# Encoder layer: the embedding gate's products in another order and by token tiles, softmax division inside the probability turn

## The chip, the cores and the metric

The kernel runs on one core of one Trainium2 chip. The metric is the device time of one launch in microseconds (us). The core has a TensorE (PE, with its weight loads as PEld), a VectorE (DVE), a ScalarE (ACT), a GpSimd (POOL) and a SyncE (SP, which here only issues DMAs). A text "L659" is line 659 of the kernel before.

## The reference

One layer on 1024 tokens of width 1024, all in float32:

```python
u = x @ w_in                                  # 2816 columns: rq, rk, rv, rg, aq, ak, av
y_ret = swish(rg) * group_norm(retention_fwd + retention_bwd)      # 8 heads, chunks of 128
y_att = softmax(window scores + alibi, with a sink logit) @ v      # 8 query, 2 key heads, blocks of 128
h = layer_norm(ALPHA * x + concat(y_ret, y_att) @ w_out)           # LN1
g = sigmoid(h @ w_ple_gate)                                        # the embedding gate
f = (silu(h @ w_ffn_gate) * (h @ w_ffn_up)) @ w_ffn_down
out = layer_norm(ALPHA * h + f + g * (p @ w_ple_proj))             # LN2
```

## The kernel before

**Arithmetic.** Large products run in a pair of shorter floats: `split` (L78-80) copies an operand on ACT to a rounded high part and subtracts on DVE for the low part, and `mm3` or `mm3c` (L83-85, L277-279) does three 512-column products for one. The in-projection, the gate, and the FFN's up and down products use a scheme that replaces the eight block products of a 2 by 2 block matrix by seven; its operands are sums of blocks, and its results are sums of products.

**Stages.** In order: the in-projection ("dense" stage, up to about 170 us), attention and retention (to 410), w_out with LN1 (to 505), the embedding gate `ple` (to 606), the FFN's gate and up products (units of four weight tiles; to about 1035), and the down product with LN2.

**Attention and retention.** Heads go in four pairs. For a pair, PE's order is written out by hand as a list of steps given to `run`: K and C are the retention's keys and their products with values (`Retention.keys`, `kv`), Q, Y, N, X its scores, outputs, norms and turns, sco(n), trn(n) and val(n) the scores, the turn and the values of attention block n (`Attention`). F is a place for filler work: `run` takes 28 steps of three products each from one queue (the rest of the in-projection and p @ w_ple_proj) and deals them over the F of a pair, in 28 groups. Only PE is ordered by hand here; a scheduler places the other engines' instructions. Scores of a block: PE, a DVE step that adds the mask and takes the maximum (L651), an ACT exponential with its sum, a DVE reciprocal, and a DVE multiplication of the 128 x 384 scores by the reciprocal (L659, 64 of them). A turn transposes the two heads' scores on PE (L667, 176 blocks of 128 x 128), into PSUM banks that `tbank` (L465) takes in rotation from "t", "t" and "mm"; "mm" is also the fillers' bank. ACT copies the result to SBUF (ptr, L669), and the values multiply it (L679). Before the first pair's scores, `first_keys` (L403) makes rounded copies of its queries and keys, 12 on ACT and 8 on DVE. `weight_sums` (L414) makes sums of the gate's weight blocks on POOL and stores them to DRAM (wsd).

**Gate.** `to_hT` (L846) transposes the normalised tokens (accs) and splits them into HB: four tiles, by half of the features and half of the tokens. `pg` (L921) loads half of a product's weights and splits them, on DVE and POOL in turn. `prod` (L949) runs one of the seven products, with the 128 rows of weights as the outer loop, four PSUM banks open, and side work between. The order is 3, 7, 1, 6, 2, 5, 4; Tokens 4 to 7 are the first block row; they are transposed beside product 7, and tokens 0 to 3, the second block row, inside the w_out loop. Sums of token blocks (`less`, TT) are DVE and POOL steps over 1024 columns of SBUF tiles. `embed_next` (L979) multiplies one gate tile by an embedding tile fetched from DRAM (pe<-ed) and adds the product to zd in DRAM; there are 16 of these, two buffers for the fetched tiles, and each use issues the next fetch on SP. Those left after the gate go one to an FFN unit. After `ple`, `ahead(2, 4)` loads and splits the first FFN weights (in_w_gu, L1088). From the gate on, all engines are ordered as the code is written.

Of the kernel before, what the change touches and what calls it, by code (L numbers as in the profile page):

```python
# [40 lines left out]
def layer(tc, xT, xn, w_first, w_mt, w_out, w_pg, w_pe, pT, w_gu, w_dn,  # L41
# [341 lines left out]
    def slope(i, g):  # L383
        return 2.0 ** -(i + 4 * g + 1)

    def conv_q(i, raw):

        qs = [bt([P, S], "aq", 3, F32R) for _ in range(2)]
        for c in hs:
            for g in range(2):  # L390
                sc_ = 0.125 / slope(i, g)
                a = slice(64 * g, 64 * g + 64)
                z = slice(64 * (1 - g), 64 * (1 - g) + 64)
                act.activation(qs[g][a, c], raw[a, c], AF.Copy, scale=sc_)
                dve.scalar_tensor_tensor(qs[g][z, c], raw[a, c], sc_, qs[g][a, c].bitcast(F32), ALU.mult, ALU.subtract)
        return qs

    k1 = [bt([P, S], f"k1{g}", dt=F32R) for g in range(2)]
    kz = [bt([P, S], f"kz{g}", dt=F32R) for g in range(2)]
    pairs = [[first[2], first[3], None]]  # L400
    for g in range(2):
        pool.memset(kz[g][64 * (1 - g):64 * (1 - g) + 64, :].bitcast(F32), 0.0)

    def first_keys():
        pairs[0][2] = conv_q(0, first[0])
        for c in hs:
            for g in range(2):
                a = slice(64 * g, 64 * g + 64)
                z = slice(64 * (1 - g), 64 * (1 - g) + 64)
                act.activation(k1[g][a, c], first[1][a, c], AF.Copy)  # L410
                dve.tensor_tensor(kz[g][a, c], first[1][a, c], k1[g][a, c].bitcast(F32), ALU.subtract)
                act.activation(k1[g][z, c], first[1][a, c], AF.Copy)
# [1202 lines left out]
```

## Time and profile before

| | |
|---|---|
| runs shown | 1275.48, 1268.9, 1267.56 us (median 1268.9) |
| profiled execution | 1273.47 us, span 1270.5 us, granted clock 0.980 |
| busy over the span | PE 1200.0, DVE 797.3, ACT 509.5, POOL 505.0 us |
| attention (168 to 410) | PE busy 221.41 of 242 us |
| gate and FFN start (505.7 to 663.3) | PE busy 119.88 of 157.6 us |

The profile is of one execution, whose time stands beside its span. Busy time over the whole span is an average over stages with different limits; the stages are read one by one below. In a row of an instruction, out<-in are the program's names; in a group's row follow the count, the busy time, the mean time of one in ns, and the idle time ahead of it with what ended it.

### The profile page before, as it was taken

The page shows a single profiled execution, that of the slowest core. Times are in us where ns is not written, and L with a number is a line of the kernel's source. Part 1 is how long each engine was busy: PE and PEld are TensorE (multiplying, and loading weights), DVE is VectorE, ACT ScalarE, POOL GpSimd, SP SyncE. Part 2 cuts the span into 40 slices and gives each one's busy share as a digit, 9 for nine tenths or more (in the row PEclk, how much of TensorE's full clock was granted, in tenths as well). Part 3 has the DMA queues.
Part 4 walks back from the last instruction along what each step waited for, and adds up shares of the span by engine and source line. Part 5 has one row for each costly group of instructions (what it writes and reads, how often), then busy time and mean ns, then how long its engine had stood idle before and what let it go on. Part 6 is the DMA issues. An engine that isn't in the chain of part 4 may idle for free.

```text
span 1270.5 us, 16734 instructions
## 1 busy us (share of the span) xinstructions
PE 1200.0 (94%) x5899; PEld 988.1 (78%) x5899; DVE 797.3 (63%) x1339; ACT 509.5 (40%) x954; POOL 505.0 (40%) x436
## 2 busy tenths in 40 slices
PE   9999979999999999997669999999999999999997
PEld 7778868787787887775458888888888888888886
DVE  7854377877685477576555455554455546875568
ACT  5432365555656312524413333332333324653442
POOL 2553023332211023226557556556556615034235
PEclk9999989999999999998889999999999999999999
DMA  5223342452311323223673322233332248999986
GB/s 216 87 99 116 122 165 79 167 199 76 126 34 67 116 100 116 100 100 93 175 163 124 125 107 78 76 112 124 125 109 75 80 155 239 373 293 220 251 202 198
DMA packets 72675, 177.40 MB, mean 140 GB/s; under 512 B 8592, under 2 KB 10768, under 8 KB 72592
## 3 DMA queue, kind: packets, MB, share of 16 engines
q1 hardware_dynamic: 61648, 155.37, 34.6%
q0 software_dynamic: 10944, 20.98, 9.6%
q8 instruction: 46, 0.75, 0.2%
q14 instruction: 37, 0.30, 0.1%
HBM read 123.10 MB, written 47.97 MB: 135 GB/s over the span
## 4 chain that ended last, share of the span: by engine, by line
PE 78%; DVE 9%; DMA 6%; ACT 3%; issue 3%; POOL 2%; SPq 0%; DVEq 0%; ACTq 0%; POOLq 0%
PE bs L279 5%; PE bs L277 5%; PE bo L277 5%; PE bs L278 5%; PE bo L279 5%; PE bo L278 5%; PE bmm L277 5%; PE bmm L278 5%; PE bmm L279 5%; PE bt L279 5%; PE bt L277 5%; PE bt L278 5%; PE bmm L83 3%; PE bmm L84 3%; PE bmm L85 2%
## 5 line engine op out<-in xcount | busy, mean ns | idle before, releaser
L1126 POOL TENSOR_TENSOR ev<-ev 128x512 f32<-128x512 f32 x33 | 54.6, 1655 | 91.4 <-DVE ev L1141 38.1
L80 DVE TENSOR_TENSOR w<-raw,w 128x512 fp32r<-128x512 f32 x53 | 47.3, 903 | 54.3 <-ACT w L79 54.2
L80 DVE TENSOR_TENSOR w<-H,w 128x512 fp32r<-128x512 f32 x44 | 41.1, 935 | 61.7 <-ACT w L79 61.7
L646 POOL COPY sc<-skb 128x1 f32<-128x1 f32 x64 | 17.3, 279 | 132.5 <-PE bt L667 45.6
L1096 POOL TENSOR_TENSOR H<-ln 128x512 f32<-128x512 f32 x22 | 28.7, 1306 | 89.3 <-DMA ln<-in_w_gu 89.3
L1130 POOL TENSOR_TENSOR ev<-ev,ev 128x512 f32<-128x512 f32 x44 | 62.7, 1437 | 2.6
L1124 ACT ACTIVATE ev<-ev 128x512 f32<-128x512 f32 x33 | 20.9, 632 | 101.9 <-DVE ev L1141 101.9
L80 DVE TENSOR_TENSOR u<-H,u 128x512 fp32r<-128x512 f32 x47 | 36.5, 776 | 37.4 <-ACT u L79 37.1
L83 PE MATMUL bmm<-H,w 128*128 128x512 f32 x112 | 49.9, 445 | 0.1
L79 ACT ACTIVATE w<-raw 128x512 fp32r<-128x512 f32 x53 | 32.5, 624 | 43.0 <-DMA raw<-in_w_gu 16.7
L655 ACT ACTIVATE sc<-sc,st 128x385 f32<-128x385 f32 (+1 forms) x64 | 37.1, 584 | 25.4 <-DVE st L653 19.6
L79 ACT ACTIVATE u<-H 128x512 fp32r<-128x512 f32 x47 | 29.6, 630 | 44.1 <-POOL H L1097 10.1
L85 PE MATMUL bmm<-H,w 128*128 128x512 f32 x112 | 44.6, 398 | 0.0
L84 PE MATMUL bmm<-H,w 128*128 128x512 f32 x112 | 44.5, 397 | 0.0
L832 POOL TENSOR_TENSOR stt<-stt,cst 128x1 f32<-128x1 f32 x8 | 11.6, 1451 | 76.7 <-DVE stt L831 70.0
L80 DVE TENSOR_TENSOR u<-raw,u 128x512 fp32r<-128x512 f32 x30 | 35.3, 1177 | 10.2 <-ACT u L79 10.2
L651 DVE CUSTOM_DVE_ANT_0 sc<-cst,bs,skb 128x384 f32<-128x384 f32 (+1 forms) x64 | 35.0, 574 | 5.0 <-PE bs L650 5.0
L1100 POOL TENSOR_TENSOR H<-raw,H 128x512 f32<-128x512 f32 x22 | 37.8, 1717 | 0.0
L79 ACT ACTIVATE w<-H 128x512 fp32r<-128x512 f32 x44 | 27.4, 622 | 22.1 <-PE bs L279 7.5
L1097 POOL TENSOR_TENSOR H<-H,raw 128x512 f32<-128x512 f32 x22 | 35.1, 1594 | 1.7
L1246 POOL DMA_DIRECT2D h0b<-in_w_dn x24 | 21.3, 900 | 31.6 <-issue 18.4
L1246 POOL DMA_DIRECT2D H<-in_w_dn x11 | 9.6, 872 | 58.3 <-DMA H<-in_w_dn 51.9
(813 smaller groups left out, 4171.6 us busy)
## 6 DMA issues: line engine op xcount, KB each, us to landing
ad<-ev SPq DMA_DIRECT2D x33, 512.0 KB, 2.6
raw<-in_w_gu SPq DMA_DIRECT2D x22, 512.0 KB, 4.4
ln<-in_w_gu SPq DMA_DIRECT2D x22, 512.0 KB, 3.6
raw<-ad SPq DMA_DIRECT2D x40, 256.0 KB, 6.0
ln<-ad SPq DMA_DIRECT2D x37, 256.0 KB, 6.4
H<-in_w_dn SPq DMA_DIRECT2D x33, 256.0 KB, 6.7
raw<-in_w_mt SPq DMA_DIRECT2D x12, 512.0 KB, 3.5
h0b<-in_w_dn POOLq DMA_DIRECT2D x24, 256.0 KB, 6.8
```

Of the source, the lines that this page charges most:

```text
L79: act.activation(hi, raw, AF.Copy)
L80: dve.tensor_tensor(lo, raw, hi.bitcast(F32), ALU.subtract)
L83: pe.matmul(o, lh, rh, start=start, stop=False)
L84: pe.matmul(o, lh, rl, start=False, stop=False)
L85: pe.matmul(o, ll, rh, start=False, stop=stop)
L277: pe.matmul(o, lh, rh, start=start, stop=False, skip_group_check=True)
L278: pe.matmul(o, lh, rl, start=False, stop=False, skip_group_check=True)
L279: pe.matmul(o, ll, rh, start=False, stop=stop, skip_group_check=True)
L655: act.activation(sc[g][:, :nk + 1], sc[g][:, :nk + 1], AF.Exp, bias=st_[:, 1, j, g:g + 1], accum_out=st_[:, 2, j, g:g + 1])
L1100: pool.tensor_tensor(s[3], a(0, 1), s[0], ALU.subtract)
L1126: pool.tensor_tensor(c[:, 1, :], c[:, 0, :], c[:, 1, :], ALU.mult)
L1130: pool.tensor_tensor(self.ev[dst][:, 0, :], left, right, op)
```

## The change

The gate's products run in the order 1, 2, 6, 7, 5, 4, 3, with the token tile as outer loop, so a tile's result is final before the next tile's begins, and its sum or sigmoid follows at once (`post`). HB of tokens 0 to 3 is the first block row. For tokens 4 to 7, `to_T` forms the block sums of one tile from the PSUM transposes while products 1 and 2 run. LN1 of a tile follows one tile later inside the w_out loop. Weights are loaded two products ahead and split one ahead; POOL does four of the splits, and the fourth block sum (t4s). All 16 embeds are on DVE, 12 of them beside products 5, 4 and 3. The first FFN weights are loaded inside product 3.

In attention the multiplication by the reciprocal goes (64 DVE steps). POOL makes a diagonal matrix of the reciprocals (dg, 32 steps of 128 x 256), and the turn is an f32 product with it in place of a transposition (176 blocks). A turn uses the two "t" banks. The first pair's queries and keys are copied in the dense stage, behind four of its last products. A block's values follow its turn by one step, and the last block's go into the next pair. The number of F in a pair is 22 for the first, and 20 for the others.

```diff
-    def first_keys():
-        pairs[0][2] = conv_q(0, first[0])
...
+    def keys(c):
+        if not k1:
+            k1.extend(kt_("k", 4) for _ in range(2))
+            kz.extend(kt_("k", 4) for _ in range(2))
+            for g in range(2):
+                pool.memset(kz[g][64 * (1 - g):64 * (1 - g) + 64, :].bitcast(F32), 0.0)
+        for g in range(2):
+            a = slice(64 * g, 64 * g + 64)
+            z = slice(64 * (1 - g), 64 * (1 - g) + 64)
+            act.activation(k1[g][a, c], first[1][a, c], AF.Copy)
+            dve.tensor_tensor(kz[g][a, c], first[1][a, c], k1[g][a, c].bitcast(F32), ALU.subtract)
+            act.activation(k1[g][z, c], first[1][a, c], AF.Copy)
+
+    def queries(c):
+        if not q0:
+            q0.extend(kt_("q", 3) for _ in range(2))
+        conv_q(0, first[0], q0, [c])
...
+            if pr is projs[-1]:
+                {5: lambda: keys(hs[0]), 2: lambda: keys(hs[1]), 7: lambda: queries(hs[0]),
+                 4: lambda: queries(hs[1])}.get(p, lambda: None)()
...
-        for p, x, y in ((5, a11, a10), (7, a10, None), (6, a00, a11), (3, a01, a00)):
-            pool.tensor_tensor(x, x, a00 if p == 7 else y, ALU.add)
-            sp.dma_start(wsd[p][q][:, c], x)
+        pool.tensor_tensor(a11, a11, a10, ALU.add)
+        pool.tensor_tensor(a10, a00, a10, ALU.subtract)
+        pool.tensor_tensor(a00, a11, a00, ALU.subtract)
+        pool.tensor_tensor(a01, a01, a00, ALU.subtract)
+
+    def weight_store(kt):
+        a, b = wsums[kt]
+        for p, x in ((5, b[:, 1, :]), (7, a[:, 1, :]), (6, a[:, 0, :]), (3, b[:, 0, :])):
+            sp.dma_start(wsd[p][kt // 2][:, hs[kt % 2]], x)
...
-            for g in range(2):
-                dve.tensor_scalar(sc[g][:, :nk], sc[g][:, :nk], st_[:, 3, j, g:g + 1], None, ALU.mult)
+            dg = self.dg[n] = bt([P, 2, P], "dg", 2)
+            pool.tensor_tensor(dg, ident.unsqueeze(1).to_broadcast([P, 2, P]),
+                               st_[:, 3, j, :].unsqueeze(2).to_broadcast([P, 2, P]), ALU.mult)
...
-                tb = tbank((P, 4, P))
+                tb = bank("t", (P, 4, P))
                 for kb in range(hi - lo):
-                    pe.transpose(tb[:, kb, :], self.sc[n][g][:, kb * P:(kb + 1) * P], ident)
+                    pe.matmul(tb[:, kb, :], self.sc[n][g][:, kb * P:(kb + 1) * P], self.dg[n][:, g, :], start=True, stop=True)
...
-                sco(3), F, wsum[0], val(0), val(1), F, trn(2), Y(0, 0), F, sco(4), F, Y(0, 1), N(0), trn(3), F, sco(5), F,
...
+            else:
+                first_steps = [val_last, K(0), X0, Q(0), F, C(0), X1, gat, F, K(1), sco(0), F]
...
+                val(1), Y(0, 0), F, trn(2), sco(4), F, val(2), Y(0, 1), N(0), ws[1], F, trn(3), sco(5), ws[2], F,
...
+            val_last = val(7)
...
+    ORDER = (1, 2, 6, 7, 5, 4, 3)
...
+    def pg_load(p):
+        src = wsd[p] if p in wsd else wblk(*{1: (0, 0), 2: (0, 1), 4: (1, 1)}[p])
+        raws[p] = [rawt(2 * HF) for _ in range(2)]
+        for q in range(2):
+            sp.dma_start(raws[p][q], src[q])
+
+    def pg_split(p):
+        k = ORDER.index(p)
+        PG[p] = [wp.tile([P, 2, HF], F32R, tag="w", bufs=4, name=nm("w")) if k % 2 == 0 else ct([P, 2, HF], "u", 4, F32R)
+                 for _ in range(4)]
+        for n, t in enumerate(PG[p]):
+            x = raws[p][n // 2][:, hs[n % 2]]
+            act.activation(t[:, 0, :], x, AF.Copy)
+            (pool if n % 2 and p in (2, 6) else dve).tensor_tensor(t[:, 1, :], x, t[:, 0, :].bitcast(F32), ALU.subtract)
...
+        if t > 4:
+            ln1_apply(t - 1)
+    pg_load(1)
+    pg_split(1)
+    pg_load(2)
+    ln1_apply(NT - 1)
...
+    def to_T(t):
+
+        b0, b1 = turn_h(t)
+        x1, x3 = (sarena[0][:, 2 * (t - 4) + q, :].rearrange("p (n c) -> p n c", n=4) for q in range(2))
+        if t < 6:
+            x2 = ct([P, 4, P], "sg", 2)
+        else:
+            if t == 6:
+                lnt.append(ct([P, 2, 4, P], "ln", 2))
+            x2 = lnt[0][:, t - 6]
+        X[t] = x1, x2, x3
+        act.activation(x3, b0, AF.Copy)
+        dve.tensor_tensor(x1, b0, hi(0, 0, t), ALU.subtract)
+        dve.tensor_tensor(x1, x1, lo(0, 0, t), ALU.subtract)
+        dve.tensor_tensor(x2, b1, x1, ALU.subtract)
+        put_h(1, 1, t, b1)
+        put(2, x2, t)
+        dve.tensor_tensor(x3, b1, x3, ALU.subtract)
+        keep_h(t)
...
-    def prod(p, bs, start, stop, side={}):
+    def prod(p, bs, start, stop, post, side=()):
...
-        for kt in range(4):
-            for k in range(4):
-                c = slice(k * P, (k + 1) * P)
+        for k in range(4):
+            c = slice(k * P, (k + 1) * P)
+            for kt in range(4):
                 mm3c(bs[k], L[:, 0, kt, c], L[:, 1, kt, c], w[kt][:, 0, :], w[kt][:, 1, :],
                      start and kt == 0, stop and kt == 3)
-            for f in side.get(kt, ()):
-                f()
+            post(k)
+            if k == 1 and n + 2 < len(ORDER):
+                pg_load(ORDER[n + 2])
+            if k < len(side):
+                for f in side[k]:
+                    f()
...
+        if used[0] < len(embs):
+            t, h, f = embs[used[0]]
+            dve.tensor_tensor(f, f, es_[used[0]], ALU.mult)
+            pool.dma_start(zd[t][:, hs[h]], f, accum_op=ALU.add)
+            used[0] += 1
+            fetch()
...
+        L = lambda f, *ts: [lambda t=t: f(t) for t in ts]
+        E = [embed_next]
         b1 = banks(MS)
-        prod(1, b1, True, False, {0: [lambda: pg(6, 0), lambda: t2(0)], 2: [lambda: pg(6, 1), lambda: t2(1)]})
-        for k in range(4):
-            dve.tensor_tensor(u[k], u[k], b1[k], ALU.subtract)
-            dve.tensor_tensor(v[k], v[k], b1[k], ALU.add)
+        s1 = quad()
+        prod(1, b1, True, False, lambda k: act.activation(s1[k], b1[k], AF.Copy), [L(to_T, 4), L(to_T, 5), L(to_T, 6)])
+        g = quad()
+        prod(2, b1, False, True, c00, [L(to_T, 7), L(t3, 4), L(t3, 5, 6), L(t3, 7)])
         by = banks(TO)
-        prod(6, by, True, False, {0: [lambda: pg(2, 0), lambda: t1(0)], 2: [lambda: pg(2, 1), lambda: t1(1)]})
-        f = quad()
-        for k in range(4):
-            dve.tensor_tensor(f[k], u[k], by[k], ALU.add)
-        for q in range(2):
-            t4s(q)
-        prod(2, b1, False, True, nextw(5))
-        for q in range(2):
-            t4(q)
-        g = quad()
-        for k in range(4):
-            act.activation(g[k], b1[k], AF.Sigmoid)
-            embed(4 + k, 0, g[k], pool)
-        prod(5, by, False, True, {0: [lambda: pg(4, 0), embed_next], 1: [embed_next], 2: [lambda: pg(4, 1), embed_next],
-                                  3: [embed_next]})
-        for k in range(4):
-            dve.tensor_tensor(v[k], v[k], by[k], ALU.subtract)
-            act.activation(v[k], v[k], AF.Sigmoid)
-            embed(k, 0, v[k], dve)
-        for k in range(4):
-            dve.tensor_tensor(u[k], u[k], by[k], ALU.add)
-            act.activation(u[k], u[k], AF.Sigmoid)
-            embed(k, 1, u[k], dve)
-        b4 = banks(MS)
-        prod(4, b4, True, True, {0: [embed_next], 1: [embed_next], 2: [embed_next], 3: [embed_next]})
-        for k in range(4):
-            dve.tensor_tensor(f[k], f[k], b4[k], ALU.add)
-            act.activation(f[k], f[k], AF.Sigmoid)
-            embed(4 + k, 1, f[k], dve)
-
-    RIGHT = {1: HB[0, 1], 2: HB[1, 1], 3: HB[1, 0]}
+        u2 = quad()
+        prod(6, by, True, False, plus(u2, s1, by), [L(t1, 4) + L(t4s, 4), L(t1, 5), L(t1, 6) + L(t4s, 5), L(t1, 7)])
+        u3 = quad()
+        prod(7, by, False, False, plus(u3, s1, by), [L(t4s, 6), L(t4, 4), L(t4s, 7) + L(t4, 5), [fetch, fetch]])
+        b5 = banks(MS)
+        prod(5, b5, True, False, gate(u3, u3, b5, 4, 1), [L(t4, 6) + E, E, L(t4, 7) + E, E])
+        prod(4, by, False, True, gate(s1, s1, by, 0, 1), [E, E, E, E])
+        prod(3, b5, False, True, gate(u2, u2, b5, 4, 0), [E, E + [lambda: ahead(2, 2)], E, E + [lambda: ahead(2, 4)]])
...
-        ple()
-        RIGHT.update({4: TT[4], 5: TT[1], 6: TT[2], 7: TT[3]})
-        sarena.append(big16((P, 8, 2, HF // 2)).bitcast(F32).rearrange("p a b c -> p a (b c)"))
-        ahead(2, 4)
+        ple(ahead)
```

Three places of the order. SP at the end of the gate and the start of the FFN (pe is a fetched embedding tile, raw and ln hold FFN weights), before:

```order
L1088 DMA raw_5313<-in_w_gu 128x1024
L1088 DMA ln_5315<-in_w_gu 128x1024
L1088 DMA raw_5322<-in_w_gu 128x1024
L1088 DMA ln_5324<-in_w_gu 128x1024
L973 DMA pe_5356<-ed 128x512
L973 DMA pe_5377<-ed 128x512
L973 DMA pe_5401<-ed 128x512
L973 DMA pe_5424<-ed 128x512
L973 DMA pe_5449<-ed 128x512
L973 DMA pe_5473<-ed 128x512
L973 DMA pe_5493<-ed 128x512
L1088 DMA raw_5497<-in_w_gu 128x1024
```

and after:

```order
L1046 DMA pe_5303<-ed 128x512
L1120 DMA raw_5305<-in_w_gu 128x1024
L1120 DMA ln_5307<-in_w_gu 128x1024
L1120 DMA raw_5314<-in_w_gu 128x1024
L1120 DMA ln_5316<-in_w_gu 128x1024
L1046 DMA pe_5343<-ed 128x512
L1046 DMA pe_5361<-ed 128x512
L1046 DMA pe_5386<-ed 128x512
L1046 DMA pe_5407<-ed 128x512
L1120 DMA raw_5509<-in_w_gu 128x1024
```

The first four FFN loads stand further back among the fetches, and four fetches instead of seven stand before the fifth.

POOL in the first pair (A are the gate's weight sums, sq and dt the retention's decay tables), before:

```order
L423 TENSOR_TENSOR A_1577<-A_1577,A_1578 128x512
L520 TENSOR_TENSOR dt_1295<-sq_1296 128x128
L423 TENSOR_TENSOR A_1578<-A_1578,A_1577 128x512
L519 TENSOR_TENSOR sq_1301<-sq_1301,masks 128x256
L520 TENSOR_TENSOR dt_1295<-sq_1301 128x128
L646 COPY sc_1499<-skb 128x1
L646 COPY sc_1500<-skb 128x1
L646 COPY sc_1556<-skb 128x1
L646 COPY sc_1557<-skb 128x1
L646 COPY sc_1630<-skb 128x1
```

and after:

```order
L541 TENSOR_TENSOR sq_1332<-sq_1332,masks 128x256
L542 TENSOR_TENSOR dt_1326<-sq_1332 128x128
L444 TENSOR_TENSOR A_1718<-A_1718,A_1717 128x512
L445 TENSOR_TENSOR A_1717<-A_1717 128x512
L446 TENSOR_TENSOR A_1717<-A_1718,A_1717 128x512
L447 TENSOR_TENSOR A_1718<-A_1718,A_1717 128x512
L681 TENSOR_TENSOR dg_1436<-cst,st_1419 128x256
L668 COPY sc_1504<-skb 128x1
L681 TENSOR_TENSOR dg_1470<-cst,st_1419 128x256
L668 COPY sc_1505<-skb 128x1
```

The first diagonals (dg) stand behind the second group of weight sums, between the one-column copies that the scores of later blocks begin with.

PE in a block's turn, before (bt and bmm are the two PSUM banks of the turn, L83 to L85 a filler, L649 and L650 the scores of a later block); the values of these two, ptr_2893 and ptr_2899, come five rows further, behind those of the block before:

```order
L667 MATMUL bmm_2889<-cst,sc_2787 128x128 x3
L667 MATMUL bt_2895<-cst,sc_2788 128x128 x3
L83 MATMUL bmm_2906<-A_2513,p_2858 128x512
L84 MATMUL bmm_2906<-A_2513,p_2858 128x512
L85 MATMUL bmm_2906<-A_2513,p_2858 128x512
L649 MATMUL bs_2914<-k_1270,aq_2456 128x384
L650 MATMUL bs_2914<-kz_1272,aq_2456 128x384
L649 MATMUL bs_2918<-k_1271,aq_2457 128x384
L650 MATMUL bs_2918<-kz_1273,aq_2457 128x384
L83 MATMUL bmm_2906<-A_2516,p_2858 128x512
L84 MATMUL bmm_2906<-A_2516,p_2858 128x512
L85 MATMUL bmm_2906<-A_2516,p_2858 128x512
```

and after (L690 is the turn, L671 and L672 the scores, L702 the values):

```order
L690 MATMUL bt_1619<-dg_1520,sc_1504 128x128 x3
L690 MATMUL bt_1625<-dg_1520,sc_1505 128x128 x3
L671 MATMUL bs_1636<-k_1220,q_1266 128x384
L672 MATMUL bs_1636<-k_1222,q_1266 128x384
L671 MATMUL bs_1640<-k_1221,q_1267 128x384
L672 MATMUL bs_1640<-k_1223,q_1267 128x384
L83 MATMUL bmm_1522<-H_350,w_1315 128x512
L84 MATMUL bmm_1522<-H_350,w_1315 128x512
L85 MATMUL bmm_1522<-H_350,w_1315 128x512
L702 MATMUL bo_1557<-ptr_1623,v_1307 64x128
L702 MATMUL bo_1557<-ptr_1629,v_1307 64x128
```

Between a block's turn and its values now stand the scores of another block and one filler group.

More of the change, by code (lines that the diff above doesn't have):

```diff
@@ L191, in right @@
             return [xs[4 * i + kt][:, e, hs[j]] for e in range(2)]
-        return [TX[{4: 4, 5: 1, 6: 2, 7: 3}[p]][:, e, kt, :] for e in range(2)]
+        return [tx({4: 4, 5: 1, 6: 2, 7: 3}[p], e, kt) for e in range(2)]
     late = []
@@ L381, in bt @@
         return bpool.tile(list(shape), dt, tag=tag, bufs=bufs, name=nm(tag))
[L383 to L389, printed above, removed]
-            for g in range(2):
[L391 to L402, printed above, removed]
-    def first_keys():
-        pairs[0][2] = conv_q(0, first[0])
[L406 to L412, printed above, removed]
+    pairs = [[first[2], first[3], q0]]
+    wsums = {}
     def weight_sums(kt):
-        a, b = atile((P, 2, HF)), atile((P, 2, HF))
+        a, b = wsums[kt] = atile((P, 2, HF)), atile((P, 2, HF))
         q, c = kt // 2, hs[kt % 2]
@@ L524, in keys @@
             i = self.i
-            tb = tbank((P, 2, P))
+            tb = bank("t", (P, 2, P))
             for j in range(2):
@@ L617, in turn @@
             ymf = self.ym[hh].rearrange("p (n h) e -> p n (h e)", h=2)
-            tb = tbank((P, 4, P))
+            tb = bank("t", (P, 4, P))
             for j in range(4):
@@ L891, in layer @@
             zpart(t, h, bs[t, h], xr)
-    for i in range(2):
-        hslot(i, 0)
+    hslot(0, 0, "h2")
+    hslot(1, 0, "h3")
     for t in range(4, NT):
@@ L946, in layer, with put @@
-    LEFT = {1: lambda: HB[0, 1], 2: lambda: HB[1, 1], 3: lambda: HB[1, 0], 4: lambda: TT[4], 5: lambda: TT[1],
+        if t > 4:
[4 more added lines that the diff above has]
+    ln1_apply(NT - 1)
+    hslot(1, 1, "h0a")
+    TT, X = {}, {}
+    cols = lambda t: slice((t % 4) * P, (t % 4 + 1) * P)
+    hi = lambda i, j, t: HB[i, j][:, 0, :, cols(t)].bitcast(F32)
+    lo = lambda i, j, t: HB[i, j][:, 1, :, cols(t)].bitcast(F32)
+    lnt = []
+    def put(n, x, t, e=None):
+        h, l = (TT[n][:, q, :, cols(t)] for q in range(2))
+        act.activation(h, x, AF.Copy)
+        (e or dve).tensor_tensor(l, x, h.bitcast(F32), ALU.subtract)
@@ new lines, in layer, with fetch, embed @@
+    es_, embs, used = [], [], [0]
+    def fetch():
+        if len(es_) < len(embs):
+            t, h, _ = embs[len(es_)]
+            e = ct([P, HF], "pe", 2)
+            sp.dma_start(e, ed[t][:, hs[h]])
+            es_.append(e)
+    def embed(t, h, f):
+        embs.append((t, h, f))
+    def embed_next():
+        if used[0] < len(embs):
[4 more added lines that the diff above has]
+            fetch()
@@ new lines, in ple, with banks, gate, post @@
+    def ple(ahead):
+        def banks(ts):
+            return [bank(t) for t in ts]
+        MS, TO = ("mm", "s", "mm", "s"), ("t", "o", "t", "o")
+        for n in (2, 1, 3):
+            TT[n] = big16((P, 2, 4, HF))
+        sarena.append(big16((P, 8, 2, HF // 2)).bitcast(F32).rearrange("p a b c -> p a (b c)"))
+        TT[4] = ct([P, 2, 4, HF], "h0b", dt=F32R)
+        def gate(r, left, right, t, h):
+            def post(k):
+                dve.tensor_tensor(r[k], left[k], right[k], ALU.add)
+                act.activation(r[k], r[k], AF.Sigmoid)
+                embed(t + k, h, r[k])
+            return post
+        def plus(r, left, right):
+            return lambda k: dve.tensor_tensor(r[k], left[k], right[k], ALU.add)
+        def c00(k):
+            act.activation(g[k], b1[k], AF.Sigmoid)
+            embed(k, 0, g[k])
+        L = lambda f, *ts: [lambda t=t: f(t) for t in ts]
+        E = [embed_next]
@@ L1366, in third @@
             pool.dma_start(x, ln2[1], accum_op=ALU.add)
-        return first, second, third, lambda: sp.dma_start(out[tile_of(t)], x)
+        return first, second, third, lambda: sp.dma_start(out[t], x)
     def tail(products):
```

208 lines of the change are left out of this document (79 added, 129 removed).

## The prediction

> **What bounds the kernel now.** I read the sums by stage first, then PE's waits by releaser, then the order of time at the two places where they pile up. PE is busy 94% of the span, so a change pays only where PE waits, runs slowly, or gets other work. By stage (span; then busy time and count of PE, PEld, DVE, ACT, POOL; then granted clock, DMA share, GB/s):
> ```profile
> core 0: us, PE busy (x) PEld busy (x) DVE busy (x) ACT busy (x) POOL busy (x), PEclk, DMA share, GB/s
> 168.00:410.00 242.00, 221.41 (x1626) 185.69 (x1625) 178.97 (x497) 142.52 (x340) 60.08 (x98) 0.98 0.33 114
> 505.70:663.30 157.60, 119.88 (x493) 95.21 (x492) 97.95 (x105) 56.10 (x89) 74.00 (x53) 0.88 0.46 126
> 725.00:750.00 25.00, 25.00 (x112) 20.71 (x111) 14.65 (x19) 7.74 (x13) 18.04 (x13) 1.00 0.09 35
> 600.00:625.00 25.00, 13.04 (x50) 9.88 (x49) 11.51 (x17) 9.78 (x17) 11.74 (x12) 0.80 0.83 211
> ```
> The undisturbed stretch gives the price of a 512-column product: 25.00 / 112 = 0.223 us. The gate with the start of the FFN (505.7 to 663.3) has 493 PE instructions, 32 of them transposes of 128 columns (about 0.107 us, below): 461 x 0.223 + 32 x 0.107 = 106 us, but it lasts 157.6. So 51 us of it is not work; if a few records are missing it is a little less. PE's waits in 500 to 675 (us, times, longest) say what they are:
> ```profile
> PE bmm L277 <- ACT w L79: 11.8, 1, 11.8
> PE bs L277 <- DVE ev L1141: 11.4, 2, 11.0
> PE bt L277 <- DVE A L1042: 5.2, 1, 5.2
> PE bt L278 <- DVE u L930: 2.6, 1, 2.6
> PE bmm L277 <- DVE h0a L855: 2.3, 2, 1.3
> ```
> These are 33 us, with the smaller ones about 38; the remaining 13 go to a slow clock (0.88 and 0.80 in the windows) and to short gaps. The two largest are not in the gate but at the first two FFN units, and a DMA queue makes both. SP's own queue, and PE in order of time:
> ```profile
> 611.32 0.43 SPq L1088 DMA_DIRECT2D raw<-in_w_gu  x1
> ...
> 614.13 30.78 SPq L973 DMA_DIRECT2D pe<-ed  x7
> 645.01 0.37 SPq L1088 DMA_DIRECT2D raw<-in_w_gu  x1
> ```
> ```profile
> 618.48 0.80 PE L277 MATMUL bmm<-h0a,w 128*128 128x512 f32 x1 [11.82 <-ACT w L79]
> 619.07 0.63 PE L278 MATMUL bmm<-h0a,w 128*128 128x512 f32 x1
> 619.50 0.63 PE L279 MATMUL bmm<-h0a,w 128*128 128x512 f32 x1
> ```
> The first FFN weights are issued at 611.32, after the whole gate, and PE starts 7.2 us later. The next pair of weights stands behind seven fetches of embedding tiles (614.13 to 645), each held until DVE has used an earlier tile; they are issued only from 645.01, and PE stands 11 us. That wait is put down to a DVE step (ev), but PE's next operands are the splits of just these weights. After a stall, products come 0.43 us apart instead of 0.223 for some 3 us.
>
> **Gate and FFN start: 51 us of excess becomes about 11.5.** Removed are the sums over 1024 columns between SBUF tiles and eight of twelve weight splits on POOL. The seven products keep their count (7 x 48 x 0.223 + 32 x 0.107 = 78.4 us of PE). Token tiles 0 to 3 come first, so product 1 no longer waits for the last LN1; each tile's sum is a step of 128 tokens, so a post overlaps the next tile. What now has to be on time is DVE:
> ```profile
> L855 DVE TENSOR_TENSOR h0a<-bmm,h0a 128x512 fp32r<-128x512 f32 x4 | 2.8, 691 | 5.2 <-ACT h0a L854 5.2
> L988 DVE TENSOR_TENSOR A<-A,pe 128x512 f32<-128x512 f32 x12 | 10.4, 870 | 9.3 <-DMA pe<-ed 9.3
> ```
> I count 24 steps in to_T, 12 puts, 20 weight splits, 20 sums behind products and 12 embeds: 76 x 0.69 + 12 x 0.87 = 63 us in 78. That fits, with the work of each product spread over its four tiles, so I leave 1.5 us of waits inside the gate (bounds: 0, or the 11 us of the smaller waits above if nothing is gained). All 12 embeds beside products 5, 4 and 3 are hidden only while DVE has this slack; without it they cost at most the 10.4 us of the row.
>
> At the FFN start the loads now stand behind tile 1 of product 3, whose length is 48 x 0.223 = 10.7 us: issue about 5.4 us before its end. The row pair above has 7.2 us from issue to PE's start, and these issues may slip behind two fetches on SP:
> ```profile
> raw<-in_w_gu SPq DMA_DIRECT2D x4, 512.0 KB, 8.6
> ```
> So PE waits 2 to 9 us; I take 6, and 2 for the second unit, whose load is issued at the end of product 3. Only four fetches stand ahead of the next pair's weights, not seven, and DVE has fewer embeds left to release them, so the 11.0 us stall goes. A stall of 6 us still slows the clock: 7 products x (0.43 - 0.223) = 1.5, with a little before it 2 us. Left are 8 + 1.5 + 2 = 11.5, so **-39.8** (bounds -30, with the full 9 + 7 us at the start and some waits kept, and -48, with nearly none).
> The Trainium skill, "TensorE: Matmul & The Clock Gate", Part 1, puts half clock after an idle window of about 3.4 us; by that rule a wait cut under 3.4 us would save these 2 us as well, and the trace agrees with the factor (0.43 against 0.223).
>
> **Attention: dearer turns, fewer switches, fewer waits.** Turns, values and a recurrence product in order of time:
> ```profile
> 312.79 0.49 PE L667 MATMUL bt<-cst,sc 128*128 128x128 f32 x3
> 313.11 0.49 PE L667 MATMUL bmm<-cst,sc 128*128 128x128 f32 x3
> 313.44 0.33 PE L598 MATMUL bo<-kv,qq 128*128 128x64 f32 x2
> ...
> 318.22 0.39 PE L591 MATMUL bo<-kv,qq 128*128 128x128 f32 x2
> 318.44 0.56 PE L587 MATMUL bo<-rv,pt 128*128 128x64 f32 x4
> ...
> 319.68 0.48 PE L83 MATMUL bmm<-A,p 128*128 128x512 f32 x1
> 320.00 0.40 PE L84 MATMUL bmm<-A,p 128*128 128x512 f32 x1
> 320.24 0.40 PE L85 MATMUL bmm<-A,p 128*128 128x512 f32 x1
> ...
> 321.98 1.53 PE L679 MATMUL bo<-ptr,av 128*64 128x128 f32 x24
> 323.44 1.16 PE L567 MATMUL bs<-rkq,rkq 64*128 64x128 f32 x16
> ```
> Six transposes take 0.65 us, 0.108 each. The new turn is an ordinary f32 product, which is recorded as two instructions. The nearest row is L591, 128 rows by 128 columns both ways: 318.22 to 318.44, 0.22 us for one product. The low bound is L679, of half the stationary columns: 1.46 us / 12 = 0.12. So 176 blocks cost 176 x (0.22 - 0.108) = **+19.7** (low +2.5). All lie on PE, which is the bound here. The first of a filler group takes 0.32 instead of 0.24; 30 fewer groups x 0.08 = **-2.4**.
> The other sides of it:
> ```profile
> L659 DVE TENSOR_SCALAR sc<-sc,st 128x384 f32<-128x384 f32 (+1 forms) x64 | 25.8, 446 | 0.5
> L423 POOL TENSOR_TENSOR A<-A,A 128x512 f32<-128x512 f32 x10 | 12.8, 1280 | 5.9 <-DMA A<-in_w_pg 5.6
> L519 POOL TENSOR_TENSOR sq<-sq,masks 128x256 f32<-128x256 f32 x7 | 5.3, 750 | 3.1 <-ACT sq L518 3.1
> ```
> 25.8 us leave DVE, which is busy 179 of 242 here and off the path; I cost that at nothing, since PE covers it. The diagonal is one POOL step of the last row's size, 32 x 0.75 = 24 us on an engine busy 60 of 242, and ready before its turn unless it stands behind weight_sums (four steps of the L423 kind). Waits now:
> ```profile
> PE bt L477 <- ACT av L478: 5.0, 1, 5.0
> PE bt L542 <- DVE kdec L531: 3.3, 4, 1.7
> PE bmm L83 <- ACT es L739: 3.2, 3, 2.4
> PE bt L667 <- DVE sc L659: 1.8, 4, 1.1
> ```
> In all PE idles 242.00 - 221.41 = 20.6 us here (first fence). The first is ACT working through twelve query and key copies of 0.63 us ahead of its own copy:
> ```profile
> 172.76 1.92 ACT L394 ACTIVATE aq<-A 64x512 fp32r<-64x512 f32 x3
> ...
> 180.90 0.57 ACT L478 ACTIVATE av<-bt 128x512 f32<-128x512 f32 x1
> ```
> The change does these in the dense stage, beside products that leave ACT room, so 5.0 goes, with up to two smaller waits for the same copies; and since the mm bank is left to the fillers, waits as the third row's 3.2 shrink. Late next are values: each now follows its own turn by one filler group and four score products (about 1.5 to 2.2 us), in which ACT copies two blocks of 0.48 us:
> ```profile
> L669 ACT ACTIVATE ptr<-bt x44: 361/475/494, 190.4 to 398.6; 128x384 f32<-128x384 f32 x32, 128x256 f32<-128x256 f32 x12
> ```
>  I keep 11 of 20.6, **-9.6** (bounds: 5 and 25 left). The 12 copies and 8 DVE steps now stand beside the last products of the dense stage; one step of 0.64 (1.92 / 3) after the last product stays open: **+0.7**, bounds -1 and +3.
>
> Sum: -39.8 + 19.7 - 2.4 - 9.6 + 0.7 = **-31.4**. The profiled execution is 1273.5 (span 1270.5 and 3.0 around it), 0.36% above the median of 1268.9; it goes to 1242.1, and the median to 1237.5, **1238 us**.
>
> **The rivals.**
> - Values wait. If ACT's two copies come late behind its queue at every one of the 32 values, by the 0.5 us of a copy, attention loses 32 x 0.5 = 16: 1254. For it: ACT is busy 143 of 242 and turns now share two banks. Against: fillers stand between. 0.12.
> - The FFN start is not mended: SP reaches the weights only when the last embed tiles are used, as now. The first stall of 11.8 and a second of 4 stay instead of 8, plus the slow clock and refill: 7.8 + 2 + 5 = 15: 1253. For it: SP still has four fetches behind the loads and several ahead. 0.10.
> - Slower than before: every turn waits for its diagonal on POOL. It decides the sign from 31.4 / 32 = 0.98 us of extra wait at each of the 32 turns, and gives slower by over 1% from (31.4 + 12.7) / 32 = 1.38; at 1.4 us it is 1238 + 45 = 1283. Against: POOL is busy 60 of 242, and its weight_sums block only 4 x 1.28 = 5.1 us four times. 0.04.
> - The turn without the transpose's own path costs four times a transpose, not twice: 4 x 0.108 = 0.43 a block, 176 x 0.32 = +57 in place of 19.7: 1275, no change. Against: the row at 318.22, where an f32 product of this size takes 0.22. 0.04. The Trainium skill, same page, Terms, gives the transpose mode as "4× faster for FP32"; by that rule this rival holds, and the row does not bear it out.
>
> **How the numbers follow.** Forecast 0.70, within 1226 to 1249 (-48 in place of -39.8, with a little of the cheaper turn, at one end; -30 with the dense end's +3 at the other). The predicted time is its own. The range 1224 to 1255 takes in the two rivals near 1254 in about half of their cases and leaves out the rest. A measurement can tell about 1%, 12.7 us, from no change. Under 1256 lie the forecast (0.70) and most of the two middle rivals: faster 0.87. The time within 1% is the fourth rival and their tail: 0.09. Slower: 0.04.
>
> **What would show it.** In the profile after: seven times about 11 us of PE in the gate and a stretch of some 118 us; the first FFN weights issued before product 3 ends; no PE wait of 11 us between the first FFN units; turn products 0.22 us apart; no twelve copies ahead of the value turn; PE's waits in attention near 11 us. Wrong would make it: turns 0.43 apart, PE waiting for dg or ptr at most turns, or in_w_gu issued behind the last fetch.

## The result and the profile after

The changed kernel takes 1257.6 us (median of 4 runs, 1254.3 to 1258.5), the kernel before 1271.9 (4 runs, 1267.6 to 1275.5): a ratio of 0.988 with a 95% interval of 0.984 to 0.993. That is 14 us faster; 31 were forecast, and the time lies 2.6 us above the range. The profiled execution went from 1273.5 to 1257.4 us, its span from 1270.5 to 1255.5.

Three points of PE's order that both kernels pass place the difference (a column is the three products of one `mm3` or `mm3c`): the start of w_out's last column moved from 503.2 to 513.7 us (**+10.5**), the end of the FFN's 60th column (180 instructions into the FFN) from 675.0 to 658.2, so the gate and the FFN's start gained **27.3**, and the start of the last column of all from 1262.0 to 1247.0, so **1.8** were lost after that. The sums by stage (same columns as in the prediction), first of the kernel before, for the gate and for the first 60 FFN columns:

```profile
503.90:606.30 102.40, 87.66 (x369) 69.87 (x367) 67.45 (x68) 40.46 (x63) 46.74 (x28) 0.92 0.31 97
606.30:675.00 68.70, 45.37 (x182) 35.95 (x181) 41.00 (x48) 19.73 (x33) 39.32 (x32) 0.85 0.61 153
```

and of the kernel after, for attention, for the gate and for the same 60 columns:

```profile
160.00:420.00 260.00, 251.43 (x1830) 214.18 (x1829) 168.02 (x438) 145.02 (x339) 82.23 (x132) 0.99 0.32 109
514.40:601.90 87.50, 81.38 (x367) 67.05 (x366) 62.87 (x91) 40.72 (x69) 26.17 (x22) 0.98 0.50 144
601.90:658.20 56.30, 46.39 (x183) 36.68 (x182) 34.68 (x41) 18.43 (x31) 35.95 (x28) 0.88 0.52 141
```

The gate fell from 102.4 to 87.5 us (78.4 without a wait, by the prediction's count), the FFN's start from 68.7 to 56.3, of which 180 x 0.223 = 40.2 are work; its clock is 0.88, after 0.85 before. PE's waits after, in 500 to 660 and then in 165 to 430:

```profile
PE bmm L288 <- ACT u L79: 7.0, 1, 7.0
PE bt L288 <- DVE A L1079: 4.7, 1, 4.7
PE bs L288 <- DVE ev L1173: 2.9, 1, 2.9
PE bo L877 <- DVE H L998: 1.4, 1, 1.4
```
```profile
PE bt L499 <- DVE A L275: 2.5, 1, 2.5
PE bo L620 <- DVE kv L579: 1.9, 1, 1.9
PE bt L690 <- POOL dg L681: 1.4, 2, 1.1
PE bo L702 <- ACT ptr L692: 0.5, 2, 0.3
```

So the waits of attention all but went, and PE is no faster there: it has more to do. In the gate one long wait is left, 4.7 us at the start of product 7 (and one of 1.4 beside product 1), and the first FFN unit still waits 7.0 us. SP's queue of the kernel after, in order of time:

```profile
586.56 15.04 SPq L1046 DMA_DIRECT2D pe<-ed  x7
601.65 0.42 SPq L1120 DMA_DIRECT2D raw<-in_w_gu  x1
```

The first FFN weights stand behind tile 1 of product 3 in the code, half-way through it, but SP issues them at 601.65, when product 3 is all but over: the fetch ahead of them in the queue waits for a buffer that DVE's embed step gives back.

### The profile page after: what moved, and what is told of

It is laid out like the page before. It is cut to its first block, busy times and chain, and to the rows that moved or that the text cites. A ratio compares the mean times of both kernels' runs of the same rounds, so it can differ in the third digit from the quotient of the medians.

```text
span 1255.5 us, 17085 instructions
## 1 busy us (share of the span) xinstructions
PE 1217.1 (97%) x6075; PEld 1008.4 (80%) x6075; DVE 774.7 (62%) x1294; ACT 511.6 (41%) x958; POOL 497.4 (40%) x455
## 4 chain that ended last, share of the span: by engine, by line
PE 79%; DVE 8%; DMA 5%; ACT 3%; issue 3%; POOL 1%; SPq 0%; DVEq 0%; ACTq 0%; POOLq 0%
PE bo L288 5%; PE bo L290 5%; PE bo L289 5%; PE bt L288 4%; PE bt L289 4%; PE bt L290 4%; PE bmm L290 4%; PE bmm L288 4%; PE bmm L289 4%; PE bs L288 4%; PE bs L290 4%; PE bs L289 4%; PE bmm L83 3%; PE bt L690 3%; PE bmm L84 3%; PE bmm L85 3%
## 5 line engine op out<-in xcount | busy, mean ns | idle before, releaser
L80 DVE TENSOR_TENSOR w<-raw,w 128x512 fp32r<-128x512 f32 x51 | 43.3, 862 | 38.0 <-ACT w L79 37.8
L681 POOL TENSOR_TENSOR dg<-cst,st 128x256 f32<-128x256 f32 x32 | 21.4, 668 | 92.4 <-DVE st L679 77.7
L80 DVE TENSOR_TENSOR u<-raw,u 128x512 fp32r<-128x512 f32 x32 | 38.8, 1215 | 18.8 <-ACT u L79 18.7
L690 PEld LDWEIGHTS bt<-dg,sc 128*128 128x128 f32 x352 | 44.0, 191 | 5.8 <-POOL dg L681 2.6
L83 PE MATMUL bmm<-H,w 128*128 128x512 f32 x112 | 48.2, 431 | 0.2 <-ACT H L79 0.2
L690 PE MATMUL bt<-dg,sc 128*128 128x128 f32 x352 | 45.0, 276 | 1.6 <-POOL dg L681 1.4
L85 PE MATMUL bmm<-H,w 128*128 128x512 f32 x112 | 44.4, 396 | 0.0
L692 ACT ACTIVATE ptr<-bt 128x384 f32<-128x384 f32 (+1 forms) x64 | 29.1, 461 | 29.7 <-PE bt L690 29.0
```

The costliest lines, as they stand in the source:

```text
L80: dve.tensor_tensor(lo, raw, hi.bitcast(F32), ALU.subtract)
L83: pe.matmul(o, lh, rh, start=start, stop=False)
L85: pe.matmul(o, ll, rh, start=False, stop=stop)
L690: pe.matmul(tb[:, kb, :], self.sc[n][g][:, kb * P:(kb + 1) * P], self.dg[n][:, g, :], start=True, stop=True)
```

## Experiments

All are edits of the changed kernel unless said otherwise. Ratios are to the kernel before; the changed kernel's own is 0.988 [0.984, 0.993]. The intervals of the runs with a few edits each overlap with it, so the time alone does not tell what an edit did; that is read from its stage in the profiled executions. These differ by themselves too: in the changed kernel and the five runs with the same attention code, w_out's last column starts between 513.7 and 515.3 us. The three runs that combine the edits lie clear of the changed kernel.

### The turn: division back on DVE

```diff
-            dg = self.dg[n] = bt([P, 2, P], "dg", 2)
-            pool.tensor_tensor(dg, ...)
+            for g in range(2):
+                dve.tensor_scalar(sc[g][:, :nk], sc[g][:, :nk], st_[:, 3, j, g:g + 1], None, ALU.mult)
...
-                    pe.matmul(tb[:, kb, :], ..., self.dg[n][:, g, :], start=True, stop=True)
+                    pe.transpose(tb[:, kb, :], ..., ident)
```

> The changed kernel with the softmax division back on DVE (64 steps) and the turn back to 176 transposes; everything else as changed. Theory of the prediction's terms: PE's turns cost 18.8 us less, DVE has room for 25.8 us more, so attention is 15 to 19 us shorter and the kernel beats both (span near 1238). Rival: the division in the turn is what took the waits out of attention (20.8 to 6.6 us of PE idle); with DVE loaded again PE waits for it at turns, recurrences and fillers: idle goes back up by 8 us or more, and the gain is under 10 us.

1250.9 us, ratio 0.984 [0.981, 0.988]; w_out ends at 509.2, 4.5 us earlier. The rival held: PE idles 19.0 us from 160 us (just ahead of the dense end) to w_out's last column where the changed kernel idles 8.8 (some 2 us of each still in the dense stage). Its longest waits there:

```profile
PE bt L564 <- DVE kdec L553: 3.8, 4, 1.6
PE bs L671 <- DVE pt L592: 3.5, 6, 0.7
PE bo L620 <- DVE kv L579: 2.8, 3, 1.3
PE bt L550 <- DVE kv L568: 2.4, 2, 1.8
```

None of these is at a turn of the probabilities (those wait 2.0 us in all). In some the division stands in DVE's order ahead of a step of the retention, which is then late, as at the longest of the first row:

```profile
242.16 2.17 DVE L681 TENSOR_SCALAR sc<-sc,st 128x256 f32<-128x256 f32 x2
244.26 0.41 DVE L553 TENSOR_TENSOR kdec<-bt,kd 128x256 f32<-128x256 f32 x1
```
```profile
244.72 0.71 PE L564 MATMUL bt<-rv,kdec 128*128 128x128 f32 x4 [1.64 <-DVE kdec L553]
```

At others, as the 1.8 us at 299.8, no division stands close ahead. With the division in the turn, then, PE waits some 10 us less, though DVE was busy only three quarters of the stage; I had costed that at nothing. But this run changes two things: DVE has 25.4 us of divisions more, and PE's turns are some 18 us shorter, so that PE reaches its other steps sooner and can wait for them longer. No run keeps the long turns with the division on DVE, so how much of the 10 us is DVE's load stays open.

### Values: two blocks in a step again

```diff
-                val(1), Y(0, 0), F, trn(2), sco(4), F, val(2), Y(0, 1), N(0), ws[1], F, ...
+                val(0), val(1), Y(0, 0), F, trn(2), sco(4), F, Y(0, 1), N(0), ws[1], F, ...
```

> The changed kernel with two blocks' values in one step again (16 value steps in place of 32; turns, scores and filler groups where they are). Theory: a value step has a fixed cost on PE whatever its length: its last record takes 0.20 us instead of 0.10, its first pair 0.06 more, and the filler ahead of it 0.33 instead of 0.24, some 0.22 us in all; 16 fewer are 3.5 us of PE, and w_out ends 3 to 4 us earlier (513.7 now). Rival: the time in the turn's results is what counts, and moving values does nothing (within 1 us), or the later values hold ACT's copies and PSUM banks and PE waits more (later by 1 us or more).

1252.9 us, ratio 0.983 [0.979, 0.987]. The dense stage happened to end 2.0 us later in the profiled execution and w_out 1.9 us earlier, so the stage between is 3.9 shorter; 3 to 4 were expected, of w_out itself. In the runs with the changed kernel's attention this stage takes 344.6 to 346.4 us, here 342.1. In order of time, a single step of the changed kernel, with its turn behind it, and a double step of this run:

```profile
322.82 0.88 PE L702 MATMUL bo<-ptr,v 128*64 128x128 f32 x12
323.63 0.49 PE L613 MATMUL bo<-kv,qq 128*128 128x128 f32 x2
...
326.22 1.50 PE L690 MATMUL bt<-dg,sc 128*128 128x128 f32 x12
327.48 0.42 PE L671 MATMUL bs<-k,q 128*128 128x384 f32 x1
```
```profile
328.50 1.53 PE L702 MATMUL bo<-ptr,v 128*64 128x128 f32 x24
329.96 1.16 PE L589 MATMUL bs<-rkq,rkq 64*128 64x128 f32 x16
```

Twelve records take 0.81 us, 24 take 1.46, not 1.62; the filler ahead pays another 0.09 for each step. And a turn of six blocks takes 1.26 us, 0.21 a block: that term of the sum was right.

### Queries and keys back in the attention list

```diff
-            if pr is projs[-1]:
-                {5: lambda: keys(hs[0]), ...}.get(p, lambda: None)()
...
+                fk = (lambda: [f(c) for f in (queries, keys) for c in hs],)
+                first_steps = [F, K(0), (turn_rv, 0), F, Q(0), (turn_rv, 1), F, fk, C(0), ...
```

> The changed kernel with the first pair's query and key copies back in the attention stage (in the list of steps, where they were before). Theory: beside the last dense products they delay DVE's sums, which makes the waits of 2.0 and 2.5 us there; without them these go, but waits of 5.0 and 1.8 us for ACT at the value turn come back: within 3 us of the changed kernel. Rival: no such waits come back, since the step list is another, and it is 4 us faster; or the first scores come late too and it is over 5 us slower.

1257.5 us, ratio 0.989 [0.985, 0.993]: no difference, but also no test. Only PE's order is by hand in that stage, and the scheduler put the copies beside the last dense products again (155 to 165 us on ACT), so neither theory was tried. What the earlier copies are worth stays open.

### In the gate: the fourth token sum, and product 7's weights

PE's 4.7 us wait ends with DVE's sum behind product 6 (L1079), which reads the PSUM bank that product 7 adds to. DVE ahead of it, and POOL beside it, in the changed kernel:

```profile
547.13 6.87 DVE L979 TENSOR_TENSOR H<-H,H 128x512 fp32r<-128x512 f32 x4 [0.57 <-ACT H L978]
553.92 2.49 DVE L913 TENSOR_TENSOR u<-raw,u 128x512 fp32r<-128x512 f32 x4
556.33 0.68 DVE L1079 TENSOR_TENSOR A<-A,bt 128x512 f32<-128x512 f32 x1
```
```profile
541.00 1.29 POOL L1009 TENSOR_TENSOR sg<-h,sg 128x512 f32<-128x512 f32 x1
...
551.85 1.60 POOL L1010 TENSOR_TENSOR ln<-ln,h 128x512 f32<-128x512 f32 x1
```

Four steps on SBUF operands take 1.72 us each while POOL makes the fourth token sum, and 0.62 each (2.49 / 4) once it is done. (The Trainium skill, "GPSIMD Engine Reference", section "Specifications", says that the two engines contend when DVE has two SBUF inputs; these rows agree and give the price.) First that sum went to DVE, beside product 7:

```diff
-        pool.tensor_tensor(x, hi(1, 0, t), x, ALU.subtract)
+        dve.tensor_tensor(x, hi(1, 0, t), x, ALU.subtract)
```

> The changed kernel with the eight POOL steps of the fourth token sum (t4s) on DVE, beside product 7 instead of product 6. Theory: PE's 4.7 us wait ahead of product 7 comes from DVE steps on two SBUF operands that take 1.72 us instead of 0.69 while POOL works (four puts, 6.87 us); without POOL they take 0.69, the wait falls to 1 to 3 us, and the time falls 2 to 6 us. Rival: product 7's weights, which reach ACT only at 551.2, hold it as long: the wait stays over 4 us, and eight more DVE steps (5.5 us) make new waits: 0 to 5 us slower.

1254.0 us, ratio 0.987 [0.982, 0.991]; the gate is 2.9 us shorter, and the wait 2.9 us, now for ACT. But the first FFN unit waits longer:

```profile
PE bmm L288 <- ACT u L79: 9.2, 1, 9.2
PE bt L288 <- ACT H L978: 2.9, 1, 2.9
```

Then, in addition, the loads of product 7's weights one token tile earlier, ahead of the stores of token tile 7:

```diff
-            if k == 1 and n + 2 < len(ORDER):
+            if k == (p != 2) and n + 2 < len(ORDER):
```

> The run before with the fourth token sum on DVE (PE's wait ahead of product 7 fell from 4.7 to 2.9 us, now put down to ACT), and the loads of product 7's weights issued one token tile earlier, ahead of the stores of token tile 7 in SP's queue. Theory: those stores (held until ACT has scaled the tile at 546) delay the load to 546.55, ACT's splits of these weights hold its other copies, and so PE; without it the wait goes under 1 us, and the gate is 3 to 4 us shorter than in that run (gate 514.8 to 599.2). Rival: the raw buffers are not free earlier, or ACT is late for other reasons: the wait stays over 2 us.

1256.5 us, ratio 0.986 [0.981, 0.990]. Product 7 waits 1.1 us, and the gate's 112 columns take 80.7 us (87.3 in the changed kernel): both causes of the wait are shown. The time hardly moves, since PE then stands at the FFN:

```profile
PE bmm L288 <- ACT u L79: 11.9, 1, 11.9
PE bs L288 <- DVE ev L1173: 4.1, 2, 2.9
```

The FFN begins at 607.8, where it began at 609.5. PE was not what set that time.

### The FFN's start: loads, embeds, and the second pair

First the loads alone, from tile 1 of product 3 to tile 0 of product 4:

```diff
-        prod(4, by, False, True, gate(s1, s1, by, 0, 1), [E, E, E, E])
+        pre = [lambda: [pairs2[0].load(m) for m in range(2)]]
+        prod(4, by, False, True, gate(s1, s1, by, 0, 1), [pre + E, E, E, E])
```

> The changed kernel with the first FFN weight loads (four of 512 KB) issued after tile 0 of product 4 instead of after tile 1 of product 3; their splits stay where they are. Theory: in the changed kernel SP issues them only at 601.65, behind a fetch of an embedding tile that waits for DVE's multiplication; so PE waits 7.0 us at the first FFN unit and then runs some 3 us at half clock. Here SP issues them some 15 us earlier, the wait is under 1 us, and the time is 8 to 12 us below the changed kernel (span 1255.5). Rival: the splits on ACT and DVE, or the 2 MB of traffic beside the embedding fetches, hold it, and PE still waits 5 us or more there or in products 4 and 3: within 3 us of the changed kernel.

1252.1 us, ratio 0.985 [0.981, 0.988]. The first unit's wait is 4.0 us and the 60th column ends at 651.7, 6.5 earlier; neither theory is quite right. Behind that 2.7 us are lost again, with one wait of PE's for DVE in the down product. SP issues the loads at 587.78, but then DVE stands at an embed whose fetch is behind them, with the splits in its order behind that:

```profile
600.45 0.69 DVE L1055 TENSOR_TENSOR A<-A,pe 128x512 f32<-128x512 f32 x1 [8.49 <-DMA pe<-ed]
```

So in the next run products 4 and 3 have no embeds (`[pre]`, and empty lists in place of E):

> The changed kernel with the first FFN loads issued after tile 0 of product 4, and no embed step in products 4 and 3 (8 of the 12 go to FFN units). Theory: the embeds are what holds the FFN: in DVE's order each waits for its fetch (8.5 us behind the FFN loads in the run with early loads), and the splits stand behind it. Without them the splits are done before product 3 ends: PE's wait at the first unit is under 1 us, no slow clock after it, and FFN's 60th product (658.2 us in the changed kernel, 651.7 with early loads alone) comes by 648 to 650. Rival: ten or more embeds in the FFN delay its first units or the second pair's loads, as before the change: a wait of 4 us or more comes back there, and nothing is gained on the early loads alone.

1252.7 us, ratio 0.983 [0.978, 0.987]. The first wait is gone, and one of 10.0 us stands at the second pair, as before the change; the 60th column ends at 656.1, so the rival held. SP here:

```profile
608.77 15.17 SPq L1046 DMA_DIRECT2D pe<-ed  x7
624.05 1.02 SPq L1121 DMA_DIRECT2D raw<-in_w_gu  x1
```

A variant with six embeds in the gate, and the second pair's loads ahead of most fetches:

```diff
             gunits[k][2]()
+            if k in (1, 4):
+                for m in range(2):
+                    pairs2[1].load(m, (k // 4,))
             embed_next()
```

> The changed kernel with six embeds in the gate (products 5 and the first two tiles of 4), then the first FFN loads, no embeds until the FFN runs, and the second pair's loads taken out of the fetches' way (raw parts after the second FFN unit, the other parts after the fifth). Theory: both FFN waits come from loads and splits that stand behind embed steps in SP's and DVE's order; with neither behind them PE waits under 1 us at the first unit and under 2 us at the second pair's (10.0 us in the run with embeds moved alone), and the 60th FFN product comes by 648 (658.2 in the changed kernel). Rival: DMA traffic (fetches, read-add-write of zd, weights) is the limit itself: the loads are only late elsewhere, waits of 5 us or more remain, and the 60th product stays after 652.

1253.3 us, ratio 0.985 [0.982, 0.987]: again no wait at the first unit, and 8.0 us at the second pair; the 60th column ends at 654.2. The rival's number, but not yet its cause.

### All together, and where the last wait came from

The variant just told, with the two edits of the gate and values in pairs:

> The same FFN start, with the gate's two edits (fourth token sum on DVE, product 7's weights loaded earlier) and two blocks' values in a step. Theory: the gains add: gate 6.6 us, FFN start some 10 us, values 2 to 4 us below the changed kernel: span near 1237, ratio to before near 0.971. Rival: the gate's gain is given back at the FFN start as it was alone (wait 7.0 to 11.9): span 1243 or more.

1247.3 us, ratio 0.980 [0.977, 0.982], span 1244.5: the attention and gate gains stay (w_out ends at 508.7, the gate takes 81.0), and the second pair's wait is 7.8. The span is nearer the rival's 1243 than the theory's 1237, but for another wait than the rival's: the first unit waits 0.5. Then the division on DVE as well:

> The run before it with the softmax division back on DVE and transposes as turns. Theory: as alone, 18.8 us less of turns on PE against some 10 us more waits: w_out ends 4 to 8 us earlier than without. Rival: with values in pairs the turns' results are needed later, so DVE's lateness hurts less, and it ends over 10 us earlier; or the waits take all of it (under 2 us).

1239.2 us, ratio 0.973 [0.970, 0.976]; w_out ends 4.9 us earlier. The wait at the second pair is now 8.9, and DVE ahead of it shows why:

```profile
612.86 0.68 DVE L80 TENSOR_TENSOR u<-H,u 128x512 fp32r<-128x512 f32 x1
619.36 0.69 DVE L1054 TENSOR_TENSOR A<-A,pe 128x512 f32<-128x512 f32 x1 [5.82 <-DMA pe<-ed]
```
```profile
PE bs L288 <- DVE ev L1173: 9.3, 2, 8.9
```

The next splits are ready on ACT since 609 and 612, and stand behind one embed. So the last run spreads the embeds:

```diff
-            embed_next()
+            if k in (0, 1, 2, 5, 7, 8, 10, 11, 13, 14):
+                embed_next()
+            if k == 5:
+                for m in range(2):
+                    pairs2[1].load(m, (1,))
```

> The run with everything (embeds one to an FFN unit, the division on DVE) with two things moved: the ten embeds left go to units 0, 1, 2, 5, 7, 8, 10, 11, 13 and 14, so that each follows its fetch by two units or more, and the second pair's remaining loads come after unit 5's embed. Theory: PE's 8.9 us wait at the second pair comes from DVE, which stands 5.8 us at an embed whose fetch is behind 1 MB of weights, with the sums and splits of the units behind it; with the fetches landed in time that wait falls under 3 us, and the span goes from 1237.1 to about 1229. Rival: the DMA engines' traffic or POOL's contention with DVE holds it: the wait stays over 6 us, wherever the embeds stand.

1231.9 us, ratio 0.968 [0.965, 0.970]: faster than both kernels. The wait at the second pair is 1.7 us, and the 60th column ends 44.9 us after the FFN's first product starts (55.0 in the run before it); that first product now waits 2.7 us:

```profile
PE bmm L288 <- ACT u L79: 2.7, 1, 2.7
PE bs L288 <- DVE ev L1173: 1.7, 1, 1.7
```

The span is 1231.9, not 1229: the stage behind, to the last column of all, is 3.9 us longer than in the run before it, with a wait of 2.1 us for DVE and slow products in the down product. Gate and FFN start in this run:

```profile
503.10:584.30 81.20, 79.82 (x367) 65.93 (x367) 60.94 (x95) 39.59 (x68) 11.22 (x10) 1.00 0.48 143
584.30:632.50 48.20, 42.47 (x184) 33.84 (x183) 34.42 (x40) 16.54 (x28) 33.07 (x26) 1.00 0.60 154
```

The clock is 1.00 in both. In the FFN's start DMA moved more per us than in the changed kernel (154 against 141 GB/s), so traffic as such was not the limit.

## Why the prediction was wrong

**The place was right, the size was not.** Against the spans' 15.0 us, the prediction had 31.4. Its gate and FFN term missed by 12.5 (-27.3 in place of -39.8), the stages ahead of the gate by 2.1 (+10.5 in place of +8.4), and 1.8 came after the 60th column, which it had at nothing (in the down product PE waits once for DVE, 1.6 us). Of the gate and the FFN's start, 25.2 us are not work after the change, where 11.5 were left: waits in the gate 6.1 for 1.5, waits at the FFN 9.9 for 8, the slow clock about 6.5 for 2, and some 2.7 of short gaps, which the sum left out.

**"That fits, with the work of each product spread over its four tiles".** The step that failed in the gate. The count of DVE's steps came out (62.9 us busy over the gate), but not when they run and at what price: beside POOL's token sum four steps cost 6.87 us, not 2.8. The forecast's upper bound, 11 us, was itself low as a count of the smaller waits: in the kernel before the gate's waits are 14.8. The runs with POOL relieved and with the weights earlier took the larger one to 2.9 and to 1.1.

**"issue about 5.4 us before its end".** The step that failed at the FFN's start. SP issued the loads at 601.65, not near 597: the rival in which "SP reaches the weights only when the last embed tiles are used" has the cause. That its 1253 came near is luck, since its waits of 11.8 and 4 us did not come. I had priced 12 embeds as DVE time "hidden only while DVE has this slack". Their price is not their 0.69 us but the wait for each fetch, which stops everything behind it on DVE and, through the buffer it holds, on SP. It was shown from three sides: loads moved, embeds moved, embeds spread. The waits themselves, 7.0 and 2.9 us against 6 and 2, were only a little off in the changed kernel; what the late issue cost is told by the run with the loads 14 us earlier, whose 60th column ends 6.5 us sooner.

**The slow clock.** 2 us were left; three stalls made about 6.5, so this term was mis-sized. After the 7.0 us wait, 13 products come 0.43 apart, not 7. The granted clock of the kernel after says when (it is the third number from the right; PE's busy time follows the stretch's length):

```profile
553.85:557.26 3.41, 0.10 (x1) 0.14 (x2) 3.41 (x7) 1.90 (x4) 0.00 (x0) 1.00 0.28 82
557.26:560.67 3.41, 3.41 (x9) 2.64 (x10) 3.41 (x7) 1.15 (x2) 0.00 (x0) 0.50 0.73 226
601.63:605.04 3.41, 0.92 (x5) 0.42 (x3) 0.00 (x0) 0.00 (x0) 0.86 (x1) 1.00 0.97 220
608.46:611.87 3.41, 2.34 (x6) 1.81 (x7) 0.69 (x1) 0.99 (x2) 1.49 (x2) 0.50 0.85 345
611.87:615.28 3.41, 3.41 (x10) 2.64 (x9) 3.11 (x4) 0.90 (x2) 3.33 (x3) 0.50 0.01 5
639.18:642.59 3.41, 1.06 (x5) 0.56 (x3) 1.54 (x2) 0.63 (x1) 3.33 (x3) 1.00 0.71 196
642.59:646.00 3.41, 2.91 (x7) 2.36 (x8) 2.16 (x3) 1.15 (x2) 3.36 (x3) 0.50 0.00 0
```

In all thirteen traces the clock changes only at marks that lie whole multiples of 3.41 us apart, and between 100 and 1200 us it stays at half for one to four such stretches. Here each half-clock spell follows a stretch in which PE worked 0.10, 0.92 or 1.06 of the 3.41 us; it goes on after one with 2.34, and ends after one with 2.91 or 3.41. What a stall costs therefore depends on where it falls between the marks: 2.85 us of waiting was followed by 6 products at half clock, 2.94 us in the run with product 7's weights earlier by none, and 2.7 us in the last run by none. The Trainium skill ("TensorE: Matmul & The Clock Gate", Part 1) asks for an idle window of about 3.4 us, and I expected none from shorter waits; the same page says that its window runs freely. The marks agree with that, but PE need not idle for the whole window: 1.06 us of work in it did not prevent the slow clock.

**Attention.** The turn's price was right (352 records at 0.106 us, +18.8 for 19.7 forecast), and so was the row it came from; the rival at four times a transposition fell. Waits fell further than I took (20.8 to 8.8 us of PE's idle time from 160 us to w_out's last column). The term "30 fewer groups x 0.08 = -2.4" had the wrong scope: the fillers did get cheaper (the first products of all `mm3` from 160 us to w_out's end, the fillers' among them, take 64.5 us from start to start, 66.8 before), but the same list doubled the value steps, and the pairing run prices that at +3.9. The rival of values that wait did not come: 0.5 us in all.

**The turn and DVE's relief belong together.** "I cost that at nothing, since PE covers it": the run with the division back has 10 us more of waits. So the division in the turn costs 18.8 us and gives back some 14, 10 of it in waits; w_out ends 4.5 and 4.9 us later for it in the two pairs of runs. That longer turns by themselves would have shortened the waits is not excluded. Of the change's parts, the gate and the FFN's start carry all of the gain.

## What to carry to other kernels

A step that waits for a transfer costs its engine's whole queue, not its own duration: place it so far behind its fetch that the transfer has landed (two FFN units in the last run), and put loads that the bound engine needs ahead of fetches that are paced by another engine's progress. When a stage's stall is removed, look at once at the next stage's start: 6.6 us taken out of the gate moved the FFN's first product by only 1.8, because its start was set by a chain of fetches and embeds. And when PE's order is rewritten, count how often it goes from one kind of product to another, not its products alone.

## What the runs showed of the hardware

A row of f32 products with 64 stationary columns (the value steps) has a fixed cost at its end and at its start: the pitch of a pair is 0.11 us inside (0.007 and 0.103 for its two records), the last record before another kind of product takes 0.20, and the 512-column product ahead of the row 0.33 instead of 0.23. An ordinary f32 product of 128 x 128 x 128 costs 0.21 us, twice a transposition of the same block (0.106). The clock's marks of 3.41 us and DVE's 1.72 us beside POOL stand above.
